# A two-layer mLSTM, GLA and sparse-attention block: projections with rows on partitions in 512 columns, weights kept by pieces, gates and w_out by blocks of rows

## Chip, cores and metric

The kernel runs on one core of a Trainium2 chip. The metric is the time of one execution in microseconds on the device, as the median of several runs. The engines are named as in the profile: PE (TensorE, with PEld for its weight loads), DVE (VectorE), ACT (ScalarE), POOL (GpSimd), SP (SyncE, which issues most of the DMAs).

## The reference

x has 512 rows (S) of 1024 (D_MODEL). Each of two layers does the following, all in float32; `split_columns` cuts the 9312 columns of the product with w_in by name.

```python
COLUMN_LAYOUT = (
    ('ml_q', 1024), ('ml_k', 1024), ('ml_v', 1024), ('ml_o', 1024), ('ml_z', 1024),
    ('ml_i', 4), ('ml_f', 4),
    ('gla_q', 256), ('gla_k', 256), ('gla_v', 512), ('gla_a', 16), ('gla_r', 512),
    ('dsa_q', 512), ('dsa_k', 512), ('dsa_v', 512), ('dsa_z', 512),
    ('idx_q', 512), ('idx_k', 64), ('idx_w', 8))

def hybrid_layer(x, ...):
    p = split_columns(rmsnorm(x, norm_g) @ w_in)
    qk = silu(causal_dwconv(concatenate([p['ml_q'], p['ml_k']]), ml_conv_w, ml_conv_b))
    mq, mk = split(qk, 2)
    hm = mlstm_chunkwise(heads(mq, 4), heads(mk, 4), heads(p['ml_v'], 4), li, lf)
    hm = hm * sigmoid(heads(p['ml_o'], 4))
    y_ml = rmsnorm(hm, ml_norm_g) * silu(p['ml_z'])
    la = log_sigmoid(p['gla_a'] @ gla_w_a + gla_b_a) / 16
    hg = gla_chunked(heads(p['gla_q'], 4), heads(p['gla_k'], 4), heads(p['gla_v'], 4), heads(la, 4))
    y_gla = rmsnorm(hg, gla_norm_g) * silu(p['gla_r'])
    dq, dk = rmsnorm(heads(p['dsa_q'], 4), dsa_q_g), rmsnorm(heads(p['dsa_k'], 4), dsa_k_g)
    hd = dsa_sparse_attention(dq, dk, heads(p['dsa_v'], 4), iq, p['idx_k'], iw, rel_bias, 128)
    y_dsa = hd * silu(p['dsa_z'])
    return x + concatenate([y_ml, y_gla, y_dsa]) @ w_out          # w_out: 2048 x 1024
```

The sparse attention scores all keys with the index heads, keeps the best 128 of each query, and attends to those with a relative bias.

## The kernel before

**Products.** Every float32 matrix product is made of three float32r products (`mm3`): a value is cut into a high part (hi) and the rest (lo), and hi x hi, hi x lo and lo x hi are summed in PSUM. x, after its norm, is transposed 128 rows at a time (`norm_in`: xs is the scaled block, psx its transposes, xhi and xlo the two parts with the 1024 inputs on partitions, 8 pieces k of 128).

**Two kinds of projection.** `proj_t` (PSUM tile pt) has the weights as the stationary operand: output columns on partitions, 512 rows of x streaming (384 in one case). It serves ml_q, ml_k, gla_q, gla_k and the index columns. `proj_n` (PSUM tile pn) has a block of 128 rows of x as the stationary operand and streams 256 weight columns, so that the rows lie on partitions; two blocks of rows stand side by side in one PSUM tile of 512. It serves ml_v, ml_o, ml_z, gla_v, gla_r and the four dsa groups, each in groups of 256 columns. Per group, pair of row blocks (pr), block (j) and k there are three matmuls. `chunks_two` does the same for the two gla_v groups, block by block, since the blocks of x become ready one after the other.

**Weights.** They are packed on the host in the order of use (`group_order`); a group is two halves of 128 x 1024 (512 KB each). A half is loaded by SP into a tile of the tag "w" (5 tiles: raw and lo), copied to float32r by ACT into the tag "hi" (4 tiles), and DVE subtracts (lo = raw - hi). `load`, `split`, `split_part`, `finish_split`, `take` and `done_with_group` keep this going: the next group's halves are split while one group is used, and tiles come back by whole groups.

**Order of the work.** A layer first does gla_v, the small columns (misc), idx_q and the GLA queries and keys, then goes through PLAN: ml heads 0 to 2, then "close" ml_z of heads 0 and 1, and so on; a close step is a gate (`y_group`: two groups of z, tanh, gating, transposes psy, parts yhi and ylo) followed by a quarter of the product with w_out (`w_out_part`, PSUM tile pw, 512 columns streaming, result added to xr). The recurrent and attention parts are background tasks: generators cut into stages that are issued between the projections' matmuls. Every engine call passes through `Meter.call`, which books it on an estimated clock of each engine (`Clock`), and at each `tick` the class `Background` issues the stages that should be ready by that clock, by priority. So the order in each engine's queue is fixed when the program is built, and all operations carry the same line, L180, in the profile. Tiles of 4 KB per partition come from the tag t4 (9), 2 KB from t2 (19), 8 KB from f8 (2).

**Names in the rows.** pn, pt, pw: see above; psx with xs, xhi, xlo: transposes of x; psy: transposes of a gated branch, of which so is mLSTM's, gv GLA's and dsa_v the attention's; cacc: the causal convolution of ml_q and ml_k (on DVE in threes); psq with qn: transposed dsa queries and keys; bs: relative bias with selection; pskd with kdn, and psst: GLA's state update; qz, psga: GLA's products inside a chunk.

Of the kernel before, what the change touches and what calls it, by code (L numbers as in the profile page):

```python
# [64 lines left out]

def group_order():
    order = []

    def cols(name, g=0):
        order.append(("in", OFF[name] + 256 * g))  # L70

    def out(q):
        order.append(("out", 512 * q, 0))
        order.append(("out", 512 * q, 512))

    def unit(kind, g):
        if kind == "dsa":
            for n in ("dsa_q", "dsa_k", "dsa_v"):
                cols(n, g)
        else:  # L80
            for n in ML_ORDER:
                cols(n, g)

    def steps(plan):
        for step in plan:
            if step[0] == "close":
                for g in range(2):
                    cols(step[1], step[2] + g)
                out(step[3])
            else:  # L90
                unit(*step)

    cols("gla_v", 0)
    cols("gla_v", 1)
    order.append(("misc",))
    cols("idx_q", 0)
    cols("idx_q", 1)
    order.append(("gqk", 0))
    order.append(("gqk", 1))
    steps(PLAN)  # L100
    return order


ML_ORDER = ("ml_o", "ml_q", "ml_k", "ml_v")
PLAN = (("ml", 0), ("ml", 1), ("ml", 2), ("close", "ml_z", 0, 0), ("ml", 3), ("close", "gla_r", 0, 2), ("dsa", 0), ("dsa", 1), ("close", "ml_z", 2, 1), ("close", "dsa_z", 0, 3))


def pack_weights(w_in, w_out):
    order = group_order()
    pack = np.zeros((DEPTH, len(order), 128, 2048), w_in.dtype)  # L110
    for layer in range(DEPTH):
        for i, spec in enumerate(order):
            dst = pack[layer, i]
            if spec[0] == "in":
                w = w_in[layer, :, spec[1]:spec[1] + 256]
                dst.reshape(128, KT, 256)[:] = w.reshape(KT, 128, 256).transpose(1, 0, 2)
            elif spec[0] == "gqk":
                d = dst.reshape(128, KT, 2, 128)
                for b, name in enumerate(("gla_q", "gla_k")):
                    w = w_in[layer, :, OFF[name] + 128 * spec[1]:OFF[name] + 128 * spec[1] + 128]  # L120
                    d[:, :, b, :] = w.reshape(KT, 128, 128).transpose(1, 0, 2)
            elif spec[0] == "out":
                w = w_out[layer, spec[1]:spec[1] + 512, spec[2]:spec[2] + 512]
                dst.reshape(128, 4, 512)[:] = w.reshape(4, 128, 512).transpose(1, 0, 2)
            else:
                d = dst[:, 0:1024].reshape(128, KT, 128)
                for name, n, at in MISC:
                    w = w_in[layer, :, OFF[name]:OFF[name] + n]
                    d[:, :, at:at + n] = w.reshape(KT, 128, n).transpose(1, 0, 2)
                dst[:, 0:1024] = d.reshape(128, 1024)  # L130
    return pack
# [34 lines left out]
class Meter:  # L166
    """Passes instructions on to an engine and books them on the engine's estimated clock (us)."""
# [98 lines left out]
class Background:  # L266
    """Tasks cut into stages: a stage is issued once what the stage before it made should be there."""
# [65 lines left out]
def hybrid_kernel(ctx, tc, a, out, dbg=None):  # L333
# [15 lines left out]
    N_T4, N_T2, N_F8, VA_BUFS = 9, 19, 2, 1  # L349
    W_BUFS, LOAD = 5, 4.5  # L350
# [19 lines left out]
    def t4(name, n=1024):  # L370
        return wk.tile([128, 1024], F32, tag="t4", name=name, bufs=N_T4)[:, 0:n]
# [3 lines left out]

    def f8(name):
        return wk.tile([128, 2048], F32R, tag="f8", name=name, bufs=N_F8)
# [35 lines left out]
    # (scale * mean + scale * eps) ** -0.5  # L413
# [4 lines left out]
    # two float32r parts of a value in PSUM, with a gain per partition and block: high first, low a stage later  # L418
# [23 lines left out]
    # one tag holds what was loaded and the low parts; a slot of it stays free while halves wait to be split  # L442
    order = [(layer, i) + spec for layer in range(DEPTH) for i, spec in enumerate(group_order())]
    halves_of = [1 if spec[2] == "misc" else 2 for spec in order]
    to_load = [(k, half) for k in range(len(order)) for half in range(halves_of[k])]
    loaded, ready, parts, half_done = {}, {}, [], []
    state = {"held": 0, "split": 0, "used": 0, "done": 0}

    def load(limit):
        while to_load and state["held"] < limit:  # L450
            state["held"] += 1
            k, half = to_load.pop(0)
            layer, i = order[k][:2]
            raw = wp.tile([128, 1024], F32, tag="w", name=f"raw{k}_{half}", bufs=W_BUFS)
            nc.sync.dma_start(raw, a["w_pack"][layer, i, :, 1024 * half:1024 * half + 1024])
            loaded[k, half] = (raw, clock.at["pe"] + LOAD)

    def split():
        k = state["split"]
        if k == len(order):  # L460
            return
        state["split"] += 1
        ready[k] = [], []
        for half in range(halves_of[k]):
            parts.append((k,) + loaded.pop((k, half)))

    def split_part():
        if half_done:
            k, raw, hi = half_done.pop()
            lo = wp.tile([128, 1024], F32R, tag="w", name=f"lo{k}", bufs=W_BUFS)  # L470
            nc.vector.tensor_sub(lo, raw, hi.bitcast(F32))
            n = {"misc": 128, "out": 512}.get(order[k][2], 256)
            for w, t in zip(ready[k], (hi, lo)):
                w.extend(t[:, c:c + n] for c in range(0, 1024, n))
            if not parts and state["split"] >= state["done"] + 2:
                load(W_BUFS)
        if parts and parts[0][2] <= clock.at["pe"]:
            k, raw, _ = parts.pop(0)
            hi = wp.tile([128, 1024], F32R, tag="hi", name=f"hi{k}", bufs=4)
            nc.scalar.activation(hi, raw, AF.Copy)  # L480
            half_done.append((k, raw, hi))

    def finish_split(k):
        while any(p[0] <= k for p in parts + half_done):
            if not half_done:
                clock.at["pe"] = max(clock.at["pe"], parts[0][2])
            split_part()

    def take(kind, at=None):
        k = state["used"]  # L490
        assert order[k][2] == kind and (at is None or order[k][3] == at), (order[k], kind, at)
        state["used"] += 1
        finish_split(k)
        return ready.pop(k)

    def done_with_group():
        finish_split(state["split"] - 1)
        state["held"] -= halves_of[state["done"]]
        state["done"] += 1
        load(W_BUFS - 1)  # L500
        split()
# [3 lines left out]
    def tick():  # L505
        split_part()
        bg.tick()
# [6 lines left out]
    def proj_t(w, blk, s0=0):  # L514
        wh, wl = w
        ps = pp("pt")
        c = slice(128 * blk, 128 * blk + 128)
        for k in range(KT):
            mm3(ps[:, s0:S], wh[k][:, c], wl[k][:, c], xhi[:, k, s0:S], xlo[:, k, s0:S], k == 0, k == KT - 1)
# [4 lines left out]
    def proj_n(w, pair):  # L524
        ps = pp("pn")
        for j in range(2):
            proj_n_half(ps, w, pair, j)
            if j == 0:
                tick()
        return ps  # L530

    def proj_n_half(ps, w, pair, j):
        wh, wl = w
        s = slice(128 * (2 * pair + j), 128 * (2 * pair + j) + 128)
        o = ps[:, 256 * j:256 * j + 256]
        for k in range(KT):
            mm3(o, xhi[:, k, s], xlo[:, k, s], wh[k], wl[k], k == 0, k == KT - 1)
            if k % TICK_K == TICK_K - 1 and k < KT - 1:
                tick()
# [816 lines left out]
```

## Time and profile before

| | |
|---|---|
| three runs | 1235.89, 1237.62, 1238.03 us; median 1237.62 |
| profiled execution, span | 1236.4 us |
| PE busy | 1215.7 us (98%) |
| DVE busy | 830.5 us (67%) |
| ACT busy | 583.2 us (47%) |
| POOL busy | 162.0 us (13%) |
| DMA | 107.98 MB, 87 GB/s mean |

The page tells the busy time of each engine and the chain of work that ended last. For the length of a matmul the start times of neighbours count, since matmuls overlap: the busy time of one is longer than the distance to the next. A bracket at the end of a timeline row, as [0.67 <-DVE lo], is the idle time of the engine before that row and what ended it. The page gives the execution's span and no other time of it; the median of the runs lies 1.2 us above the span.

### The profile page before, as it was taken

What the parts mean: (1) busy time and instruction counts of PE and PEld (TensorE: products, weight loads), DVE (VectorE), ACT (ScalarE), POOL (GpSimd) and SP (SyncE); (2) the same over time, 40 slices, a digit from 0 to 9 for tenths busy, and PEclk for the clock granted to TensorE, in tenths of its full rate; (3) what the DMA queues carried; (4) which work ended last, traced back from release to release, by engine and by line L of the source; (5) the groups of instructions that cost most, each with busy time, mean ns of one, the idle gap of its engine ahead of it and who ended that gap; (6) DMA issues with size and microseconds to landing.
All of it is one profiled execution on the core that took longest, in us unless ns stands there. A gap on an engine that the chain in (4) does not pass through costs nothing.

```text
span 1236.4 us, 20867 instructions
## 1 busy us (share of the span) xinstructions
PE 1215.7 (98%) x8308; PEld 1095.3 (89%) x8308; DVE 830.5 (67%) x1618; ACT 583.2 (47%) x1214; POOL 162.0 (13%) x293
## 2 busy tenths in 40 slices
PE   6999999999999999999999999999999999999998
PEld 6978889899889898998898889898988998989997
DVE  5479869796887844364556978888888875234643
ACT  6564546444153265542357544564442443554321
POOL 2003112300000013200010121031210000122000
PEclk9999999999999999999999999999999999999999
DMA  4333222222222223323223223122222322313222
GB/s 160 107 108 100 87 69 78 69 78 69 83 97 96 76 71 109 112 69 102 69 70 120 69 71 106 57 93 77 69 67 71 111 69 92 123 52 116 67 83 102
DMA packets 35169, 107.98 MB, mean 87 GB/s; under 512 B 5028, under 2 KB 8388, under 8 KB 35072
## 3 DMA queue, kind: packets, MB, share of 16 engines
q1 hardware_dynamic: 33136, 104.89, 26.0%
q8 instruction: 65, 1.06, 0.4%
q0 software_dynamic: 1200, 1.36, 0.3%
q10 hardware_dynamic: 736, 0.41, 0.1%
q14 instruction: 32, 0.26, 0.1%
HBM read 104.48 MB, written 3.43 MB: 87 GB/s over the span
## 4 chain that ended last, share of the span: by engine, by line
PE 93%; DVE 2%; ACT 2%; DMA 1%; POOL 1%; issue 1%; SPq 0%; DVEq 0%; POOLq 0%
PE pn L180 42%; PE pt L180 22%; PE pw L180 14%; PE psS L180 2%; PE pom L180 2%; PE pod L180 2%; PE psga L180 1%; PE pss L180 1%; PE pog L180 1%; PE psy L180 1%; DMA bs<-skew 1%; POOL bs L180 1%; PE psl L180 1%; DVE lo L180 1%; ACT xhi L180 1%
## 5 line engine op out<-in xcount | busy, mean ns | idle before, releaser
L180 PE MATMUL pn<-hi,xhi 128*128 128x256 f32 x1536 | 445.2, 290 | 0.0
L180 PE MATMUL pn<-hi,xlo 128*128 128x256 f32 x1536 | 434.4, 283 | 1.0 <-DVE xlo L180 1.0
L180 PE MATMUL pn<-lo,xhi 128*128 128x256 f32 x1536 | 433.6, 282 | 1.3 <-DVE lo L180 1.3
L180 DVE TENSOR_TENSOR lo<-raw,hi 128x1024 fp32r<-128x1024 f32 x178 | 221.9, 1247 | 184.4 <-ACT hi L180 178.1
L180 PEld LDWEIGHTS pn<-lo,xhi 128*128 128x128 f32 x1536 | 291.6, 190 | 4.0 <-DVE lo L180 1.7
L180 PEld LDWEIGHTS pn<-hi,xhi 128*128 128x128 f32 x1536 | 289.9, 189 | 4.4 <-PE psl L180 1.0
L180 PEld LDWEIGHTS pn<-hi,xlo 128*128 128x128 f32 x1536 | 290.3, 189 | 1.5 <-DVE xlo L180 1.5
L180 ACT ACTIVATE hi<-raw 128x1024 fp32r<-128x1024 f32 x178 | 188.1, 1057 | 117.2 <-DMA raw<-w_pack 89.4
L180 PE MATMUL pt<-xhi,hi 128*128 128x512 f32 (+1 forms) x400 | 158.8, 397 | 0.0
L180 PE MATMUL pt<-xlo,hi 128*128 128x512 f32 (+1 forms) x400 | 154.5, 386 | 0.0
L180 PE MATMUL pt<-xhi,lo 128*128 128x512 f32 (+1 forms) x400 | 154.5, 386 | 0.0
L180 PE MATMUL pw<-hi,yhi 128*128 128x512 f32 x256 | 102.2, 399 | 0.0
L180 PE MATMUL pw<-hi,ylo 128*128 128x512 f32 x256 | 101.6, 397 | 0.0
L180 PE MATMUL pw<-lo,yhi 128*128 128x512 f32 x256 | 101.4, 396 | 0.0
L180 PEld LDWEIGHTS pt<-xhi,hi 128*128 128x128 f32 x400 | 75.2, 188 | 17.6 <-issue 4.2
L180 PEld LDWEIGHTS pt<-xhi,lo 128*128 128x128 f32 x400 | 75.3, 188 | 15.3
L180 PEld LDWEIGHTS pt<-xlo,hi 128*128 128x128 f32 x400 | 75.4, 189 | 12.6
L180 DVE TENSOR_TENSOR xr<-pw,xr 128x512 f32<-128x512 f32 x64 | 44.1, 689 | 51.0 <-PE pw L180 50.9
L180 DVE SCALAR_TENSOR_TENSOR cacc<-cbuf,pv,cacc 128x512 f32<-128x512 f32 x96 | 74.5, 776 | 2.5 <-ACT cacc L180 0.2
L180 ACT ACTIVATE th<-pn 128x512 f32<-128x512 f32 x32 | 19.2, 599 | 86.7 <-PE pn L180 86.7
L180 PEld LDWEIGHTS pw<-hi,ylo 128*128 128x128 f32 x256 | 48.2, 188 | 12.6 <-DVE ylo L180 1.2
L180 ACT ACTIVATE cbuf<-pt 128x512 f32<-128x512 f32 x32 | 19.1, 597 | 84.0 <-PE pt L180 79.7
(187 smaller groups left out, 1694.9 us busy)
## 6 DMA issues: line engine op xcount, KB each, us to landing
raw<-w_pack SPq DMA_DIRECT2D x178, 512.0 KB, 3.9
xr<-x SPq DMA_DIRECT2D x4, 512.0 KB, 7.7
negm<-negm SPq DMA_DIRECT2D x8, 256.0 KB, 5.2
bs<-skew SPq DMA_DIRECT2D x8, 256.0 KB, 6.1
out_dram<-xr SPq DMA_DIRECT2D x8, 256.0 KB, 2.0
bs<-skew SPq DMA_DIRECT2D x8, 192.0 KB, 6.3
skew<-flat POOLq DMA_DIRECT2D x1, 1280.0 KB, 17.9
bs<-skew SPq DMA_DIRECT2D x8, 128.0 KB, 5.5
```

Source lines behind the costliest of these rows:

```text
L180: return f(*args, **kw)
```

## The change

1. `wide` takes the place of `proj_n`, `chunks_n`, `chunks_two` and `keep_n`. A wide step is two groups of 256 columns side by side, so that one matmul streams 512 columns for one block of 128 rows (sb). The groups paired are gla_v 0 and 1, ml_o and ml_v of a head, dsa_q and dsa_k of two heads, dsa_v 0 and 1, and the two groups of every close step. Blocks 0 and 1 each go through the four weight pieces (two k's each); blocks 2 and 3 alternate piece by piece, and a piece is given back after block 3. For gla_v all four blocks go one after the other (`before` drains the norm of the block).
2. Weights are kept as `Piece`s of 128 x 1024 with one tag "w" of 11 tiles for raw, hi and lo, of which at most 3 are raw (`make_room`, `prepare`, `need`, `take`, `give_back`). The tags "hi" and f8 are gone; t4 has 11 tiles, from which iq, ik, ml_q, ml_k, yhi and ylo now come.
3. What follows a projection works by block of rows for both groups: `y_part` (gate), `qk_part` (query and key norm), the evacuations of gla_v and dsa_v, gate and values of mLSTM. The mLSTM head's order is q, k, (o, v) instead of o, q, k, v; the dsa order is q and k of group 0, v of both, q and k of group 1.
4. `w_out_part` runs by pairs of row blocks: both halves of the columns for blocks 0 and 1, then both for 2 and 3, and each block waits for its own gate task only. Before, all four blocks went through the first half, then the second.

```diff
+    def make_room(most=RAWS):
+        while to_load and state["raw"] < most:
+            if state["used"] + 1 > W_BUFS - (2 if any(p.hi is None for p in wanted) or not held else 0):
+                break
...
+    def prepare():
         if half_done:
...
+            p = half_done.pop()
+            lo = w_tile("lo", F32R)
+            nc.vector.tensor_sub(lo, p.raw, p.hi.bitcast(F32))
+            state["used"] -= 1
+            state["raw"] -= 1
...
+            make_room()
+        if to_split and to_split[0].loaded <= clock.at["pe"] and state["used"] + 2 <= W_BUFS:
+            p = to_split.pop(0)
+            state["used"] += 2
+            p.hi = w_tile("hi", F32R)
+            nc.scalar.activation(p.hi, p.raw, AF.Copy)
+            half_done.append(p)
...
+    def wide(pieces, f, before=None):
+        pss = {}
+
+        def part(sb, i):
+            if i == 0:
+                if before:
+                    before(sb)
+                pss[sb] = pp("pn")
+            s = slice(128 * sb, 128 * sb + 128)
+            wh, wl = need(pieces[i])
+            for j in range(2):
+                k = 2 * i + j
+                mm3(pss[sb], xhi[:, k, s], xlo[:, k, s], wh[j], wl[j], k == 0, k == KT - 1)
+            if sb == NB - 1:
+                give_back()
+            if i == 3:
+                f(sb, pss.pop(sb))
             tick()
...
+        lone = NB if before else NB - 2
+        for sb in range(lone):
+            for i in range(4):
+                part(sb, i)
+        if not before:
+            for i in range(4):
+                for sb in range(lone, NB):
+                    part(sb, i)
...
-            for half in range(2):
-                if half:
-                    ws.append(take("out", 512 * q))
-                for sb in range(NB):
-                    chunk(sb, half)
...
+            for pr in range(2):
+                for half in range(2):
+                    for sb in (2 * pr, 2 * pr + 1):
+                        chunk(sb, half)
...
-        def keep_gv(g, pr, ps):
-            nc.scalar.activation(gv[g][:, 2 * pr:2 * pr + 2, :], blocks(ps, 2), AF.Copy)
+        def keep_gv(sb, ps):
+            for g in range(2):
+                nc.scalar.activation(gv[g][:, sb, :], ps[:, 256 * g:256 * g + 256], AF.Copy)
...
-        chunks_two("gla_v", keep_gv, lambda sb: bg.drain(norms[sb]))
+        wide(take("wide", OFF["gla_v"]), keep_gv, lambda sb: bg.drain(norms[sb]))
```

In the whole program the matmuls of pn go from 4608 with 256 columns to 2304 with 512.

ACT at the start of the program, from the last weight copy of the first group on. Before (zw is a part of the GLA gate's weights, gv the evacuation of the first projection):

```order
L180 ACTIVATE hi_184<-raw_0_115 128x1024
L180 ACTIVATE xs,rx<-xr 128x1024
L180 ACTIVATE hi_203<-raw_1_117 128x1024
L180 ACTIVATE zw<-wa 16x256 x2
L180 ACTIVATE xs<-xr,rx 128x1024
L180 ACTIVATE xhi<-psx,pv 128x128 x8
L180 ACTIVATE xs<-xr,rx 128x1024 x2
L180 ACTIVATE gv<-pn 128x512
L180 ACTIVATE xhi<-psx,pv 128x128 x16
```

and in the changed kernel, from the same operation on (xs,rx squares block 1 of x):

```order
L178 ACTIVATE xs,rx<-xr 128x1024
L178 ACTIVATE zw<-wa 16x256 x2
L178 ACTIVATE gv<-pn 128x256 x2
L178 ACTIVATE xs<-xr,rx 128x1024 x2
L178 ACTIVATE xhi<-psx,pv 128x128 x8
L178 ACTIVATE xs<-xr,rx 128x1024
L178 ACTIVATE xhi<-psx,pv 128x128 x16
```

The evacuation gv of block 0 moved ahead of the scaling xs of blocks 1 and 2, and the fourth copy of weights moved up, out of this stretch.

PE around GLA's state update (pskd and psst) of the first pair of heads of a layer. Before:

```order
L180 MATMUL pskd<-ident,za 128x128 x3
L180 MATMUL pt<-xhi,hi_986 128x512
L180 MATMUL pt<-xlo,hi_986 128x512
L180 MATMUL pt<-xhi,lo_1005 128x512
L180 MATMUL pt<-xhi,hi_986 128x512
L180 MATMUL pt<-xlo,hi_986 128x512
L180 MATMUL pt<-xhi,lo_1005 128x512
L180 MATMUL psst<-gv,kdn 64x128 x6
```

and in the changed kernel:

```order
L178 MATMUL pt<-xhi,hi 128x512
L178 MATMUL pt<-xlo,hi 128x512
L178 MATMUL pt<-xhi,lo 128x512
L178 MATMUL pskd<-ident,za 128x128 x3
L178 MATMUL psst<-gv,kdn 64x128 x6
L178 MATMUL pt<-xhi,hi 128x512
```

The six projections that stood between pskd and psst are now ahead of pskd.

DVE in the changed kernel during the first head's convolutions, numbers kept (acc3 with m8 is the search for the best keys):

```order
L178 SCALAR_TENSOR_TENSOR cacc_1694<-cbuf_1691,pv_112,cacc_1694 128x512 x3
L178 MAX m8_1745<-acc3_638 128x8
L178 MATCH_REPLACE acc3_638<-m8_1745,acc3_638 128x512
L178 MAX m8_1748<-acc3_638 128x8
L178 MATCH_REPLACE acc3_638<-m8_1748,acc3_638 128x512
L178 TENSOR_TENSOR lo_1757<-raw_1456,hi_1737 128x1024
L178 TENSOR_TENSOR lo_1790<-raw_1586,hi_1774 128x1024
L178 TENSOR_TENSOR ml_q_1525<-cacc_1598,ml_q_1524 128x512
```

and before, in the same stage (dec and qz belong to GLA):

```order
L180 SCALAR_TENSOR_TENSOR cacc_1290<-cbuf_1287,cacc_1290 128x512
L180 SCALAR_TENSOR_TENSOR cacc_1354<-cbuf_1351,pv_112,cacc_1354 128x512 x3
L180 COPY_PREDICATED att_1211<-lev_106,psga_1381 64x8x2x16 x2
L180 TENSOR_TENSOR ml_q_1235<-cacc_1290,ml_q_1234 128x512
L180 TENSOR_TENSOR lo11_1429<-raw11_0_1358,hi11_1413 128x1024
L180 TENSOR_TENSOR dec_1297<-dec_1297,gk_705 128x32x8
L180 TENSOR_TENSOR qz1_101<-dec_1297,gq_704 64x256 x2
```

Two lo's of the changed kernel stand next to each other behind a convolution triple and a search step; before, other work lies between one lo and the next.

## Rows read from the trace of the kernel before

**Rows 1.** The page: busy us (share) and instructions; the chain that ended last.

```profile
PE 1215.7 (98%) x8308; PEld 1095.3 (89%) x8308; DVE 830.5 (67%) x1618; ACT 583.2 (47%) x1214; POOL 162.0 (13%) x293
...
PE 93%; DVE 2%; ACT 2%; DMA 1%; POOL 1%; issue 1%; SPq 0%; DVEq 0%; POOLq 0%
```

**Rows 2.** PE's waits: us in total, times, longest us.

```profile
PE psx L180 <- ACT xs L180: 9.5, 1, 9.5
PE psq L180 <- ACT qn L180: 2.8, 2, 2.0
PE pn L180 <- DVE lo L180: 1.3, 2, 0.7
PE pn L180 <- DVE xlo L180: 1.0, 2, 0.7
PE psga L180 <- DVE qz L180: 0.8, 2, 0.6
PE psy L180 <- DVE dsa_v L180: 0.6, 2, 0.3
PE psy L180 <- DVE so L180: 0.5, 2, 0.2
```

**Rows 3.** The page's groups: busy us, mean ns of one, then idle before and releaser.

```profile
L180 PE MATMUL pn<-hi,xhi 128*128 128x256 f32 x1536 | 445.2, 290 | 0.0
...
L180 DVE TENSOR_TENSOR lo<-raw,hi 128x1024 fp32r<-128x1024 f32 x178 | 221.9, 1247 | 184.4 <-ACT hi L180 178.1
...
L180 ACT ACTIVATE hi<-raw 128x1024 fp32r<-128x1024 f32 x178 | 188.1, 1057 | 117.2 <-DMA raw<-w_pack 89.4
```

**Rows 4.** Chain of waits, long pieces of PE: start us, us, what.

```profile
313.42 15.25 PE pw L180 x64
...
948.89 22.49 PE pt L180 x96
...
1184.99 11.52 PE pn L180 x96
```

**Rows 5.** Windows (behind a wait, ml, dsa): busy us by engine, PEclk, DMA share.

```profile
1090.00:1094.00 4.00, 4.00 (x24) 4.00 (x23) 0.35 (x1) 0.91 (x3) 0.00 (x0) 0.57 0.05 11
...
175.00:325.00 150.00, 149.88 (x1048) 134.18 (x1048) 123.15 (x231) 75.89 (x164) 26.73 (x47) 1.00 0.22 71
...
425.00:550.00 125.00, 123.81 (x977) 118.09 (x976) 58.61 (x167) 65.37 (x189) 24.13 (x32) 1.00 0.29 93
```

**Rows 6.** Chain of waits at the start, between two projections.

```profile
19.24 0.45 PE psx L180 x4
...
19.72 0.48 ACT xhi L180 x2
...
20.89 0.36 DVE xlo L180
...
21.30 2.90 PE pn L180 x22
```

**Rows 7.** ACT's timeline at the start: start us, us, operation.

```profile
21.73 2.24 ACT L180 ACTIVATE xs<-xr,rx 128x1024 f32<-128x1024 f32 x2
24.23 0.60 ACT L180 ACTIVATE gv<-pn 128x512 f32<-128x512 f32 x1 [0.27 <-PE pn L180]
```

**Rows 8.** DVE's timeline in an ml stretch.

```profile
185.80 1.23 DVE L180 TENSOR_TENSOR lo<-raw,hi 128x1024 fp32r<-128x1024 f32 x1 [0.90 <-ACT hi L180]
186.94 2.32 DVE L180 SCALAR_TENSOR_TENSOR cacc<-cbuf,pv,cacc 128x512 f32<-128x512 f32 x3
```

**Rows 9.** PE's timeline at the border between the layers.

```profile
626.75 0.39 PE L180 MATMUL pn<-lo,xhi 128*128 128x256 f32 x1 [0.67 <-DVE lo L180]
...
630.01 0.39 PE L180 MATMUL pn<-lo,xhi 128*128 128x256 f32 x1 [0.68 <-DVE lo L180]
```

**Rows 10.** The operations on tile pskd: ns min/median/max, first and last start.

```profile
L180 ACT ACTIVATE kdn<-pskd x4: 471/486/492, 112.3 to 834.7; 128x384 f32<-128x384 f32 x4
```

**Rows 11.** Chain of waits around the bias sums of the second layer.

```profile
1081.26 4.83 POOL bs L180 x6
...
1087.50 1.28 ACT qn L180 x4
```

More of the change, by code (lines that the diff above doesn't have):

```diff
@@ L96, in group_order, with wide @@
[L96 to L100, printed above, removed]
-    return order
-ML_ORDER = ("ml_o", "ml_q", "ml_k", "ml_v")
-PLAN = (("ml", 0), ("ml", 1), ("ml", 2), ("close", "ml_z", 0, 0), ("ml", 3), ("close", "gla_r", 0, 2), ("dsa", 0), ("dsa", 1), ("close", "ml_z", 2, 1), ("close", "dsa_z", 0, 3))
+    def wide(*names):
+        order.append(("wide",) + tuple(OFF[n] + 256 * g for n, g in names))
+    wide(("gla_v", 0), ("gla_v", 1))
@@ new lines, in group_order @@
+    order.append(("misc",))
+    for g in range(2):
+        order.append(("in", OFF["idx_q"] + 256 * g))
+    for g in range(2):
+        order.append(("gqk", g))
+    for kind, *args in PLAN:
+        if kind == "ml":
+            for n in ("ml_q", "ml_k"):
+                order.append(("in", OFF[n] + 256 * args[0]))
+            wide(("ml_o", args[0]), ("ml_v", args[0]))
+        elif kind == "dsa_qk":
+            wide(("dsa_q", args[0]), ("dsa_k", args[0]))
+        elif kind == "dsa_v":
+            wide(("dsa_v", 0), ("dsa_v", 1))
+        else:
+            wide((args[0], args[1]), (args[0], args[1] + 1))
+            order.append(("out", 512 * args[2]))
@@ L108, in pack_weights @@
+    return order
+PIECES = {"wide": 4, "out": 4, "in": 2, "gqk": 2, "misc": 1}
+WIDTH = {"wide": 512, "out": 512, "in": 256, "gqk": 256, "misc": 128}
 def pack_weights(w_in, w_out):
     order = group_order()
-    pack = np.zeros((DEPTH, len(order), 128, 2048), w_in.dtype)
+    pack = np.zeros((DEPTH, sum(PIECES[spec[0]] for spec in order), 128, 1024), w_in.dtype)
     for layer in range(DEPTH):
[L112 to L124, printed above, removed]
-            else:
[L126 to L130, printed above, removed]
@@ L439, in split_task @@
             low_part(ps, hi, lo)
[L443 to L467, printed above, removed]
-        if half_done:
[L469 to L481, printed above, removed]
@@ L494, in take, with give_back @@
[L494 to L501, printed above, removed]
+        spec, pieces = units[state["unit"]]
+        assert spec[0] == kind and (at is None or spec[1] == at), (spec, kind, at)
+        state["unit"] += 1
+        wanted.extend(pieces)
+        held.extend(pieces)
+        return pieces
+    def give_back():
+        p = held.pop(0)
+        wanted.remove(p)
+        state["used"] -= 2
+        make_room()
@@ L518, in proj_t @@
         for k in range(KT):
-            mm3(ps[:, s0:S], wh[k][:, c], wl[k][:, c], xhi[:, k, s0:S], xlo[:, k, s0:S], k == 0, k == KT - 1)
+            n = KT // len(pieces)
+            wh, wl = need(pieces[k // n])
+            mm3(ps[:, s0:S], wh[k % n][:, c], wl[k % n][:, c], xhi[:, k, s0:S], xlo[:, k, s0:S], k == 0, k == KT - 1)
+            if last and k % n == n - 1:
+                give_back()
             if k % TICK_T == TICK_T - 1 and k < KT - 1:
@@ L522, in proj_t @@
         return ps
[L524 to L539, printed above, removed]
@@ L724, in y_group, with part @@
         def y_group(name, hns, g0=0):
             yt, tasks = [], []
-            def part(g, pr, ps):
-                tasks.append(bg.start(y_part(yt, hns[g], ps, 2 * g, pr), "y"))
-            for g in range(2):
-                chunks_n(name, g0 + g, lambda pr, ps: part(g, pr, ps))
+            def part(sb, ps):
+                tasks.append(bg.start(y_part(yt, hns, ps, sb), "y"))
+            wide(take("wide", OFF[name] + 256 * g0), part)
             return yt, tasks
         def w_out_part(q, yt, tasks, after=None):
-            ws = [take("out", 512 * q)]
+            pieces = take("out", 512 * q)
```

331 lines of the change are left out of this document (159 added, 172 removed).

## The prediction

> **What bounds the kernel now.** I read the page's busy times and chain first, then TensorE's waits, the page's costliest groups, and the long pieces of the chain. TensorE is busy for 1215.7 of 1236.4 us, and 93% of the chain that ended last is its matmuls; VectorE and ScalarE stand at 67% and 47% [rows 1]. So time is won or lost in two ways only: the columns that TensorE streams take another time, or TensorE waits more or less. The waits of TensorE sum to 16.5 us, of which 9.5 us is the first load, and the rest is a handful of waits under 1 us and two of about 1.4 us [rows 2]. The profile shows no recurring wait in the middle stretch that the change could remove. What a column costs is read from long undisturbed runs of matmuls in the chain of waits, since the busy time of one matmul (290 ns for 256 columns, [rows 3]) contains the overlap with its neighbours. There, 96 matmuls of 256 columns take 11.52 us (120.0 ns each) and 96 of 512 columns take 22.49 us (234.3 ns each) [rows 4]. Both are at full clock: the granted clock is 1.00 in the wide stretches, and lower in a stretch of 4 us behind one wait [rows 5].
>
> **Columns (the gain).** The change turns 4608 matmuls of 256 columns (three forms of 1536, of which [rows 3] shows one) into 2304 of 512. Two small ones cost 240.0 ns, one wide one 234.3 (22.49 / 96 = 0.23427), so each pair saves 5.73 ns, and 2304 pairs **-13.2 us**. The bound on the other side is the slowest 512-column run in the chain, 64 matmuls in 15.25 us, 238.3 ns [rows 4]: then 1.7 ns x 2304 = -3.9 us. I take the first, because the run of projections (pt) with 512 columns and the same three products, back to back, is nearest to what the new ones are; the slower run is in w_out, between whose chunks other work stands.
>
> The Trainium skill (TensorE: Matmul & The Clock Gate, "Wait — 56ns, not 53.3ns?") puts a warm matmul at columns by 2.4 GHz plus about 2.5 ns whatever its width. By that, two halves would differ from one whole by the 2.5 ns alone, and the gain would be 2304 x 2.5 = 5.8 us, an estimate from that page. The rows here give 120.0 and 234.3 ns and so a larger fixed part; the measurement decides, and the sum does without the page.
>
> **The start.** Before, ScalarE scales block 1 of x ahead of the first evacuation of a projection, and TensorE loses 2.06 us between its transposes of block 1 (19.24) and the next projection (21.30), [rows 6]. In the new order of ScalarE both evacuations of block 0's projection stand ahead of the scaling of blocks 1 and 2, and the evacuations wait for TensorE's last matmul of block 0. From that matmul on, the chain is: two evacuations (one of 512 columns takes 0.60, [rows 7]; two of 256 I put at 0.8), two scalings 2.24 [rows 7], the first half of xhi 1.15 (19.72 to 20.87) and xlo 0.36 [rows 6], and 0.5 for the handoffs: 5.0 us. Against 2.06, and less 0.43 for four transposes of block 2 that now lie inside the wait, that is **+2.5 us** (0 if the real wait is hidden as before, +3.5 if the fourth weight piece is late too).
>
> **Weights.** Loads are as many as before, 178 of 512 KB, with the same 178 hi copies on ScalarE (1057 ns) and lo differences on VectorE (1247 ns) [rows 3]. What changes is when they are issued. Before, two groups' worth of halves lie ready and lo of a half is in most cases issued 6 us or more ahead of its first use. Now a piece must find a free slot of 11, and counted in TensorE's new order 27 of 178 have 3.1 us or less between lo's issue and first use (12 before); 22 of these are the last piece of a wide group, with 13 wide matmuls (3.04 us) ahead, and 18 (4.2 us) between hi's issue and use. The bare chain is hi 1.06 [rows 3] and lo 1.23 [rows 8], 2.3 us, which fits. It doesn't fit where a convolution triple of 2.32 us stands ahead of lo on VectorE [rows 8]: 1.06 + 2.32 + 1.25 = 4.6 us, 0.4 us over. VectorE is busy 82% in the ml stretch but 47% in the dsa stretch [rows 5], so I count the eight ml_o with ml_v pairs, take six of them as hit: 6 x 0.4 = **+2.5 us**. Bounds: 0 (all hidden; before, 12 with such leads gave two waits) and 27 x 0.4 = +11. Behind a late lo nothing but TensorE itself waits; its later background work comes later by the same amount.
>
> **At the layer border** two waits for lo, 0.67 and 0.68 us [rows 9], came from both new blocks' transposes being squeezed between first-use pieces. With w_out by blocks of rows, the norms of blocks 0 and 1 are issued half a w_out earlier, and the wide group's pieces are prepared before: **-1.3 us** (-1.3 to 0).
>
> **Small waits.** (a) w_out's chunks take the halves of a pair of row blocks together, so the gated rows 2 and 3 have four chunks of 12 x 0.234 (11.2 us) as cover instead of two (5.6); the wait psy for so disappears, **-0.5** [rows 2]. The transposes for dsa, gated per block, now follow the last dsa_v product by 1.4 us for five groups instead of two; at 0.3 us each, as the rows have it [rows 2], **+0.9** (0 to 2.5). (b) In the gla stage pskd is directly followed by psst once a layer, where six projections (1.4 us) stood between; psst needs ScalarE's kdn, 0.486 us [rows 10], and with handoffs I put it at 0.8 each: **+1.6** (0 to 2.4). (c) gla's qz waits (0.8 now, [rows 2]): **+0.5** (0 to 2). (d) psq's wait (2.0 us at the longest, [rows 2]) comes behind POOL's bias sums, 4.83 us in the chain [rows 11]; the matmuls in front of it are in the same arrangement of psl, projections and psst, so I take 0, with 1.7 either way, since the granted clock behind that wait sank to 0.57 over 4 us [rows 5].
>
> **Costs taken as nothing:** 120 more small ScalarE and 80 more VectorE operations (evacuation, gating and norms by block) lie on engines with 53% and 33% free [rows 1]. They are hidden by TensorE's projections; without that cover the ScalarE ones, at up to the 0.60 us of a 512-column evacuation [rows 7], would be 72 us. Stores and tail are as before.
>
> **The sum.** -13.2 + 2.5 + 2.5 - 1.3 + 0.9 - 0.5 + 1.6 + 0.5 = -7.0. Against the profiled execution of 1236.4 that is 1229.4; the median of the three runs lies 1.2 above that span, so **1230.6 us**.
>
> **Rivals.**
> A, everything hidden: the planner's cover suffices, the start chain overlaps, and only the columns and the vanished waits count: 1236.4 - 13.2 - 1.8 + 1.2 = 1223. For it: TensorE waits almost nowhere now, though 12 pieces have short leads. Against it: the order on ScalarE at the start leaves little room.
> B, the fixed cost per matmul is smaller than the runs suggest: at 238.3 ns the gain is 3.9 us instead of 13.2, and with the same added waits of 6.2 the time is 1236.4 - 3.9 + 6.2 + 1.2 = 1240, or 1238 if the waits are a third lower. For it: the spread of 512-column runs, 234.3 to 238.3 [rows 4]. By the fixed 2.5 ns of the page named above the same sum would be 1238, on this side too.
> C, just-in-time weights take the gain and more (slower): every last piece of a group waits, because its hi can be written only once TensorE gives back the slot, and VectorE has work queued. Without my lo term the forecast is -9.5; it ends over +2.5 (0.2%) when lo waits pass 12.0 us, that is 0.44 us on each of 27 pieces. At 0.7 us each, as the lo waits at the border show [rows 9], it is 18.9 us and 1236.4 - 9.5 + 18.9 + 1.2 = 1247. For it: ScalarE's hi is already what VectorE waits for, in 178 of its 184 us before lo [rows 3]. Against it: the new chain of 2.3 us fits into 3.04 to 4.2.
>
> **How the numbers follow.** Forecast, 1226 to 1235: 0.50. A: 0.18. B: 0.10. C: 0.16. No net effect through something not seen here: 0.06. A measurement of this kernel can tell about 0.2% from no change, so faster means under 1235.1 and slower over 1240.1: faster 0.68, same 0.16, slower 0.16. The bounds all at their low ends give 1221, at their high ends 1256. The range goes from 1220 (the low end less the scatter of 1 us of the runs), takes in A and B, and ends in the near part of C at 1242, which leaves most of C outside.
>
> **What would show it.** The pn matmuls should number 2304 and run at 234 ns start to start in an undisturbed stretch. In TensorE's waits, psx should have a second entry near 5 us, lo some ten entries of under 1 us, psst one or two for kdn, and the border's lo waits none. The forecast is wrong if pn runs at 238 ns or more (B), if lo waits sum to over 10 us (C), or if the granted clock sinks behind the new waits, which none of the terms contain.

## The result, and the profile after

The changed kernel takes 1229.86 us (median of 5 runs, 1229.35 to 1233.38), the kernel before, in the runs beside it, 1238.03 us (5 runs). The ratio is 0.9933, with a 95% interval from 0.9916 to 0.9951: faster by 8.2 us, clear of the noise. The forecast was 1230.6. The execution that was profiled took 1229.57 us with a span of 1227.9, so 1.7 us lie outside the span, where the prediction had put 1.2.

The page of the changed kernel, engines and three groups (busy us, mean ns of one, idle before and releaser); to be held against [rows 1] and [rows 3]:

```profile
PE 1200.6 (98%) x6004; PEld 970.6 (79%) x6004; DVE 836.3 (68%) x1698; ACT 601.7 (49%) x1334; POOL 165.3 (13%) x309
...
L178 DVE TENSOR_TENSOR lo<-raw,hi 128x1024 fp32r<-128x1024 f32 x178 | 219.4, 1232 | 171.1 <-ACT hi L178 169.2
L178 PE MATMUL pn<-hi,xhi 128*128 128x512 f32 x768 | 314.5, 410 | 0.0
...
L178 ACT ACTIVATE hi<-raw 128x1024 fp32r<-128x1024 f32 x178 | 188.7, 1060 | 197.1 <-PE pn L178 100.1
```

There are 768 matmuls of each form in place of 1536, as announced. The weight copy hi now waits for PE (100.1 us, the slot that is given back) where it waited for its DMA before [rows 3].

PE's waits in the changed kernel: us in total, times, longest. They sum to 23.4 us, against 16.5 [rows 2]:

```profile
PE psx L178 <- ACT xs L178: 10.3, 2, 8.4
PE psq L178 <- ACT qn L178: 3.5, 2, 1.8
PE pst L178 <- ACT bs L178: 2.7, 4, 0.9
PE pn L178 <- DVE lo L178: 2.5, 4, 1.3
PE psS L178 <- DVE ml_k L178: 1.6, 2, 0.9
PE pskd L178 <- DVE za L178: 1.4, 1, 1.4
PE psst L178 <- ACT kdn L178: 1.2, 2, 0.6
PE pod L178 <- ACT pT L178: 0.2, 1, 0.2
```

Long pieces of PE in the chain of the changed kernel (start us, us, what); they answer to [rows 4]:

```profile
933.96 22.48 PE pt L178 x96
956.44 14.01 PE pn L178 x60
...
1015.99 16.36 PE pw L178 x72
```

pn takes 14.01 / 60 = 233.5 ns, pt 234.2 as before. But pw takes 16.36 / 72 = 227.2 ns. In the kernel before, an undisturbed run of 72 of them reads

```profile
1020.73 16.86 PE pw L180 x72
```

which is 234.2 ns. The prediction did not have it that the matmuls of w_out, which keep their count and shape, would each become 7 ns shorter. Summed from start to start over the whole trace they fall from 181.6 to 176.6 us. In the 181.6 are 0.6 us that TensorE waited for dsa_v (psy, [rows 2]) right behind a matmul of w_out; without them the matmuls gave **4.4 us**, about half of the whole result. Much of what follows is about this.

### The profile page after: what moved, and what is told of

It is laid out like the page before. It is cut to its first block, busy times and chain, and to the rows that moved or that the text cites. A ratio compares the mean times of both kernels' runs of the same rounds, so it can differ in the third digit from the quotient of the medians.

```text
span 1227.9 us, 16538 instructions
## 1 busy us (share of the span) xinstructions
PE 1200.6 (98%) x6004; PEld 970.6 (79%) x6004; DVE 836.3 (68%) x1698; ACT 601.7 (49%) x1334; POOL 165.3 (13%) x309
## 5 line engine op out<-in xcount | busy, mean ns | idle before, releaser
L178 DVE TENSOR_TENSOR lo<-raw,hi 128x1024 fp32r<-128x1024 f32 x178 | 219.4, 1232 | 171.1 <-ACT hi L178 169.2
L178 PE MATMUL pn<-hi,xhi 128*128 128x512 f32 x768 | 314.5, 410 | 0.0
L178 PE MATMUL pn<-lo,xhi 128*128 128x512 f32 x768 | 306.2, 399 | 2.5 <-DVE lo L178 2.5
L178 PE MATMUL pn<-hi,xlo 128*128 128x512 f32 x768 | 305.0, 397 | 0.0
L178 ACT ACTIVATE hi<-raw 128x1024 fp32r<-128x1024 f32 x178 | 188.7, 1060 | 197.1 <-PE pn L178 100.1
L178 PEld LDWEIGHTS pn<-lo,xhi 128*128 128x128 f32 x768 | 145.5, 189 | 37.3 <-DVE lo L178 5.5
L178 PEld LDWEIGHTS pn<-hi,xlo 128*128 128x128 f32 x768 | 145.1, 189 | 35.5 <-DVE xlo L178 1.0
L178 PEld LDWEIGHTS pn<-hi,xhi 128*128 128x128 f32 x768 | 145.6, 190 | 32.9 <-PE psl L178 0.5
L178 DVE SCALAR_TENSOR_TENSOR cacc<-cbuf,pv,cacc 128x512 f32<-128x512 f32 x96 | 72.0, 750 | 2.5
L178 DVE MAX8 m<-acc 128x8 f32<-128x512 f32 (+2 forms) x96 | 53.5, 558 | 3.2 <-POOL acc L178 1.5
L178 PEld LDWEIGHTS pw<-lo,yhi 128*128 128x128 f32 x256 | 48.1, 188 | 9.5
```

What stands on the lines that cost most here:

```text
L178: return f(*args, **kw)
```

## Experiments

All are compared with 1229.86 us of the changed kernel, and each had the kernel before beside it (1238.6 to 1239.0 in those runs). The ratios are to the kernel before.

### Why w_out became faster: where the operands begin

What the change did to w_out's operands is to move them. Their tiles yhi and ylo came from the 8 KB tiles before, and come from the 4 KB tiles now. By the addresses that the built program gives its tiles, which stand in no trace, the starts modulo 512 bytes are:

| kernel | xhi, xlo | weights | yhi, ylo | distance in pn, pt | distance in pw |
|---|---|---|---|---|---|
| before | 224 | 320 | 416 | 96 | 96 |
| changed | 224 | 320 | 320 | 96 | 0 |

(pn and pw have x or y as the stationary operand and the weights streaming, pt the other way round. All steps inside these tiles are multiples of 512 bytes.) Four runs change the starts alone, with unused tiles as padding.

First run:

```diff
+    const.tile([128, 8], F32, name="pad0")
     xhi = const.tile([128, KT, S], F32R, name="xhi")
     xlo = const.tile([128, KT, S], F32R, name="xlo")
+    const.tile([128, 8], F32, name="pad1")
```

> The changed kernel with two unused tiles of 32 bytes per partition, one ahead of xhi and one behind xlo, so that xhi and xlo begin at multiples of 64 bytes (36064 and 52448 are 32 over one) and everything behind them keeps its place modulo 64. Why: w_out's matmuls run at 234 ns start to start before and 227 after; its stationary parts yhi and ylo moved from addresses 32 over a multiple of 64 to multiples of 64, as the weights are, while xhi and xlo are 32 over in both. Theory 1 (address): pn goes from 233.3 to about 227 ns (2304 x 6.6 = 15 us) and pt from 234 to about 227 (1008 x 7 = 7 us and a little in the 384 columns): about 1207 us. Theory 2 (the cadence belongs to the order of the product, w_out by pairs of blocks): pn and pt stay at 233 to 234, 1230 us.

Measured: 1227.93 us (ratio 0.9917, 0.9898 to 0.9935). Neither theory: the mean time from start to start in undisturbed stretches went from 233.4 to 232.6 ns for pn and from 233.9 to 232.6 for pt, not to 227. Modulo 64 the operands then stood alike, modulo 512 they were 128 apart.

Second run:

```diff
     make_room(2)
+    wp.tile([128, 8], F32, tag="pad", name="pad", bufs=1)
     params.append(load_parameters(0))
```

> The changed kernel with one unused tile of 32 bytes per partition behind the weights' tiles, so that all tiles of t4, yhi and ylo among them, begin 32 bytes over a multiple of 64; the weights, xhi and xlo keep their addresses. Theory 1 (address): pw goes from 227 back to about 234 ns, 768 x 6.5 = +5 us, 1235 us; pn and pt unchanged. Theory 2 (order of w_out): pw stays at 227, 1230 us.

Measured: 1233.85 us (0.9962, 0.9946 to 0.9979), 4.0 us more. Its chain shows pn as it was and pw slow again, 16.79 / 72 = 233.2 ns:

```profile
960.77 14.01 PE pn L178 x60
...
1020.37 16.79 PE pw L178 x72
```

The order of w_out's work is the same in both, so the address is the cause, and 32 bytes are enough.

Third run, the same tile ahead of the weights' tiles:

```diff
+    wp.tile([128, 8], F32, tag="pad", name="pad", bufs=1)
+
     def make_room(most=RAWS):
```

> The changed kernel with the unused tile of 32 bytes ahead of the weights' tiles: weights, yhi and ylo, xhi and xlo all begin 32 bytes over a multiple of 64. If what counts is that the two operands stand alike (relative), pn, pt and pw all run at 227 ns: 1230 - 22 = 1208 us. If each operand has to begin at a multiple of 64 (absolute), all are slow: pw 234, pn 233 or more, 1235 us or more. By theory 2 nothing moves, 1230 us.

Measured: 1227.28 us (0.9912, 0.9894 to 0.9929), neither of the two figures, since the tile also left pn and pt with a distance, 128 in place of 96. pw stays fast although weights, yhi and ylo all begin 32 bytes over a multiple of 64; pn and pt read as in the first run. Chain of waits, pt 233.2 and pw 227.5 ns:

```profile
932.23 22.39 PE pt L178 x96
...
1014.02 16.38 PE pw L178 x72
```

So it is the distance between the two operands that counts, not where each of them begins. Why it does, no run shows.

Fourth run, distance 0 everywhere (all four at 448 modulo 512):

```diff
+    lev = const.tile([128, len(LEVELS), 32], U8, name="lev")
     xhi = const.tile([128, KT, S], F32R, name="xhi")
     xlo = const.tile([128, KT, S], F32R, name="xlo")
+    const.tile([128, 32], F32, name="pad")
...
-    lev = const.tile([128, len(LEVELS), 32], U8, name="lev")
```

> The changed kernel with lev (224 bytes) moved ahead of xhi and an unused tile of 128 bytes behind xlo: xhi, xlo, the weights, yhi and ylo now all begin at 448 over a multiple of 512 bytes. The runs before showed that the distance between the two operands counts: alike, w_out's matmuls take 227 ns, 32 bytes apart 233; in the runs where xhi and the weights stood 128 bytes apart modulo 512, pn and pt went only from 233.3 and 233.8 to 232.6. Theory 1 (the distance counts modulo 512 or the like, as in w_out, where it is 0): pn and pt go to 227 ns, 2304 x 6.6 + 1008 x 7.1 = 22 us, about 1207 us. Theory 2 (64 or 128 bytes are all that counts, the rest belongs to the kind of product): as in the run with 64, 232.6 ns and 1228 us.

Measured: 1217.11 us (0.9823, 0.9808 to 0.9838), 12.75 us less than the changed kernel. All three kinds of product now run alike, 226.7, 226.7 and 226.9 ns by the chain:

```profile
924.23 21.76 PE pt L178 x96
945.99 13.60 PE pn L178 x60
...
1004.47 16.34 PE pw L178 x72
```

Theory 1 holds for the mechanism. The gain is less than its 22 us for two reasons that the trace shows. After an interruption up to some ten matmuls pass before the short time sets in, so the means are 228.0 (pn) and 228.5 (pt). Counted for each matmul from its start to the start of the next, less idle time and what half the clock cost, pn falls by 11.8 us and pt by 5.0, together 16.8. And the faster PE waits more: its waits grow from 23.4 to 27.1 us. 16.8 less 3.7 is 13.1; the spans differ by 13.3, the medians by 12.75.

Fifth run, the kernel before with the same edit:

> The kernel before with the same two edits, so that xhi and xlo begin alike with the weights modulo 512; yhi and ylo keep their distance from them. pt should go from 234 to 227 by theory 1 (1008 x 7 = -7 us). For the 256 columns of pn: if a matmul's loss by the distance is one per matmul, 4608 x 6.6 = -30 us more, 1201 us, and the wider matmuls of the change would be worth nothing; if it grows with the columns, 4608 x 3.3 = -15 us, 1216 us; if 256 columns are free of it, 1231 us. By theory 2 all stays at 1237 us.

Measured: 1232.47 us (0.9952, 0.9934 to 0.997), 6.5 us less than the kernel before in the same runs. Its chain:

```profile
945.13 21.79 PE pt L180 x96
966.92 17.27 PE pn L180 x144
...
1016.19 16.87 PE pw L180 x72
```

pt falls to 227.0 ns; pw, whose operands remain apart, stays at 234.3; pn with 256 columns stays at 119.9. So the 256-column matmuls were free of the loss on average, and the gain of the wider ones was held down by it: 2 x 119.9 - 233.5 = 6.3 ns a pair where the operands stand apart, 2 x 119.9 - 226.7 = 13.1 ns where they stand alike.

### What the columns are worth

```diff
+    def halved(ps, lh, ll, rh, rl, first, last):
+        for l, r in ((lh, rh), (lh, rl), (ll, rh)):
+            whole = first and l is lh and r is rh or last and l is ll
+            for c in (slice(0, 512),) if whole else (slice(0, 256), slice(256, 512)):
+                nc.tensor.matmul(ps[:, c], lhsT=l, rhs=r[:, c], start=first and whole, stop=last and whole)
...
-                mm3(pss[sb], xhi[:, k, s], xlo[:, k, s], wh[j], wl[j], k == 0, k == KT - 1)
+                halved(pss[sb], xhi[:, k, s], xlo[:, k, s], wh[j], wl[j], k == 0, k == KT - 1)
```

> The changed kernel with each 512-column matmul of a wide step cut into two of 256, save the first and the last of the 24 of a block: 2112 of 2304 become 4224 with 256 columns; order, pieces and background stay. If the gain of the prediction is that of the columns (2 x 119.9 against 233.3 ns, 6.5 ns a pair), the time rises by 2112 x 6.5 = 13.7 us to 1243 us. Rival: the columns are worth little and the gain came from w_out and the order, then 1230 to 1233 us.

Measured: 1241.05 us (1.0021, 1.0011 to 1.0031), 11.2 us more than the changed kernel. The columns were worth that much, and without them the change would have been slightly slower than before. Counted from start to start as for the fourth run, pn takes 11.8 us more in its trace, not the 13.7 of undisturbed stretches. The longer work also covers waits: PE's waits sum to 20.4 us there against 23.4 (lo 0.8 against 2.5, psq 2.3 against 3.5, psS 0.6 against 1.6). Two more stretches of 3.4 us at half clock in that execution cost about what those waits gave. Each matmul here has its own weight load, 8116 of both in that run against 6004, so the run doesn't tell the width from the number of loads.

The same cut with the operands alike:

> The changed kernel with both edits: operands alike modulo 512, and each wide matmul cut into two of 256 columns (2112 of 2304). Beside the run with 512 columns and the same addresses it gives what the width is worth where the distance costs nothing: 0 if two small ones cost as much as one wide one at 227 ns (113.4 each), 2112 x (2 x 119.8 - 227) = 27 us if 256 columns keep 119.8 ns.

Measured: 1235.41 us (0.9974, 0.9964 to 0.9985), 18.3 us over the run with 512 columns and the same addresses. That is between the two figures: pn takes 21.7 us more in the trace, waits 4.1 us less, and half clock costs 3.2 us more. The width and the addresses belong together: 11.2 us apart, 18.3 us alike.

### The start

In the changed kernel the chain at the start is the one that the prediction drew. ACT's timeline and then PE's (start us, us, operation, idle before and what ended it):

```profile
17.11 0.85 ACT L178 ACTIVATE zw<-wa 16x256 fp32r<-16x256 f32 x2 [2.50 <-DMA wa<-gla_w_a]
17.99 0.66 ACT L178 ACTIVATE gv<-pn 128x256 f32<-128x256 f32 x2
18.67 2.19 ACT L178 ACTIVATE xs<-xr,rx 128x1024 f32<-128x1024 f32 x2
```

```profile
19.87 1.97 PE L178 MATMUL psx<-ident,xs 128*128 128x128 f32 x12 [1.92 <-ACT xs L178]
21.49 0.78 PE L178 MATMUL pn<-hi,xhi 128*128 128x512 f32 x1
```

The evacuation gv stands ahead of the scaling xs, and PE waits for xs.

```diff
+    def scaled(sb):
+        while not norms[sb]["done"] and norms[sb].get("steps", 0) < 3:
+            bg.step(norms[sb])
...
             if i == 3:
+                if before and sb + 1 < NB:
+                    scaled(sb + 1)
                 f(sb, pss.pop(sb))
...
-        t_zw = bg.add(rank_weights())
+        t_zw = bg.add(rank_weights(), None, 0.0 if layer else 24.0)
```

> The changed kernel with another order on ScalarE at the start: the next block of x is scaled ahead of the evacuation of the projection of the block before, and the parts of the GLA gate's weights (zw) come later. In the changed kernel TensorE waits 1.92 us for the scaling of block 1, and the chain from its last projection of block 0 (17.9) to the next (21.5) is 3.6 us, against 2.1 before. If that wait is the order's, it goes and the chain returns to about 2 us: -1.5 us, 1228.3 us. Rival: the wait is that of the data (x or its norm late), then the time stays at 1229.9 us.

Measured: 1229.4 us (0.992, 0.9906 to 0.9935), no difference that can be told from 1229.86. In the trace the wait falls to 1.08 us and everything from 41 to 480 us comes 1.7 us earlier; the changed kernel then catches up. The windows (busy us of the engines, granted clock, DMA share, GB/s) show how, first of the changed kernel, then of this run:

```profile
22.00:26.00 4.00, 4.00 (x16) 2.96 (x15) 3.06 (x12) 3.96 (x13) 0.00 (x0) 0.68 0.00 2
492.00:496.00 4.00, 3.67 (x19) 2.74 (x20) 0.35 (x1) 3.29 (x10) 0.00 (x0) 1.00 0.02 4
```

```profile
22.00:26.00 4.00, 4.00 (x23) 3.32 (x22) 0.98 (x4) 2.19 (x4) 0.00 (x0) 1.00 0.00 0
492.00:496.00 4.00, 4.00 (x15) 3.54 (x16) 0.35 (x1) 1.70 (x5) 0.00 (x0) 0.57 0.02 4
```

The changed kernel's execution has a stretch at the lower clock behind the start and none at 492; the other has it the other way round. Both are 3.4 us at half the full clock, 1.7 us of work. So the lead of 1.7 us is that stretch and no more: of the order itself (the wait 0.84 us shorter, a new one of 0.44 us for xlo, restarts) nothing is left at 41 us. Whether the edit decides which pauses are followed by the low clock is not shown. The mean granted clock also differs between executions of one kernel: it was 0.992 to 0.997 in the five of the changed kernel.

### psq, and sums moved to another engine

In the changed kernel the norm rq of the last block stands behind eight bias sums on GpSimd, and ACT waits for it; the first two rows are POOL's timeline, then ACT's:

```profile
484.26 6.06 POOL L178 TENSOR_TENSOR bs<-bs,sel 128x512 f32<-128x512 f32 x8 [27.91 <-DMA bs<-skew]
490.40 0.19 POOL L178 TENSOR_SCALAR rq<-rq 128x4 f32<-128x4 f32 x1
```

```profile
491.73 1.28 ACT L178 ACTIVATE qn<-qn,rq 128x128 f32<-128x128 f32 x4 [3.42 <-POOL rq L178]
```

```diff
-            nc.gpsimd.tensor_tensor(bs, bs, selt[i], op=OP.add)
+            (nc.vector if hh else nc.gpsimd).tensor_tensor(bs, bs, selt[i], op=OP.add)
```

> The changed kernel with every second sum of bias and selection (bs) on VectorE in place of GpSimd. In the changed kernel the norm of the last block of dsa queries and keys (rq, 1.2 us on GpSimd) stands behind eight such sums (6.06 us), ScalarE waits 3.4 us for it, and TensorE then 1.75 us at psq, in each layer (0.8 and 2.0 before). If the sums are the cause, the psq waits go (3.5 us in all), and with them perhaps the stretch of 3.4 us at half clock that follows one of them (1.7 us): 1224.5 to 1226.5 us. Rival: TensorE then waits at the next place (the transposes of the probabilities, pst, 2.7 us now) for the sums that VectorE does later, and the time stays within 1 us of 1229.9.

Measured: 1230.72 us (0.9935, 0.9921 to 0.9949), the rival. psq's wait is gone, and pst's has grown from 2.7 to 8.1; PE's waits, then DVE's timeline:

```profile
PE psx L178 <- ACT xs L178: 11.1, 2, 8.2
PE pst L178 <- ACT bs L178: 8.1, 2, 4.1
```

```profile
485.94 0.91 DVE L178 TENSOR_TENSOR bs<-bs,sel 128x512 f32<-128x512 f32 x1 [5.11 <-DMA bs<-skew]
487.38 2.17 DVE L178 TENSOR_TENSOR bs<-bs,sel 128x384 f32<-128x384 f32 x3 [0.54 <-DMA bs<-skew]
```

VectorE now waits for the bias's DMA and does four sums before it comes to the maxima that the exponentials wait for. The profiled execution was the slowest of six (1232.97 us, mean granted clock 0.991, the others 0.994), with three stretches of 6.8 us at half clock where the changed kernel's had two of 3.4; in the other five, too, the clock was below the 0.996 to 0.997 of four of the changed kernel's five.

### The order of w_out

```diff
-            for pr in range(2):
-                for half in range(2):
-                    for sb in (2 * pr, 2 * pr + 1):
-                        chunk(sb, half)
+            for half in range(2):
+                for sb in range(NB):
+                    chunk(sb, half)
```

> The changed kernel with w_out in the order of before: all four blocks of rows through the first half of the columns, then through the second. The prediction gave the order by pairs 0.5 us for the gated so and 1.3 us at the border of the layers. If that was right, the psy waits for so come back (0.5 us) and the lo wait at the border (0.86 us left in the changed kernel) grows to 1.3 or more: 1231 to 1232 us. Rival: the border's lo wait has another cause and the order is worth nothing, 1229.9 us. The 227 ns of w_out's matmuls should stay either way, since the addresses stay.

Measured: 1234.83 us (0.9966, 0.9955 to 0.9977), 5.0 us more. The waits of PE that differ:

```profile
PE pw L178 <- DVE ylo L178: 3.3, 5, 1.0
...
PE pn L178 <- DVE lo L178: 1.6, 3, 1.2
```

w_out waits for ylo of the last gated blocks, 3.3 us that the order by pairs covers. The profiled execution, whose span is 6.0 us longer, also has two more stretches of 3.4 us at half clock than that of the changed kernel, which would be 3.4 us. How much of the 5.0 us is the order's own is therefore between 3.3 us, less what the border gains, and the whole. pw kept its 227 ns. And the lo wait at the border of the layers (0.86 us in the changed kernel) is absent here: with the old order there is none, so there the order by pairs costs.

### Together

> Operands alike modulo 512 bytes (1217.1 us alone) and the order at the start (1229.4 alone; in its trace 1.7 us ahead of the changed kernel up to 480 us, and level with it after a stretch of 3.4 us at half clock that the changed kernel's profiled execution did not have there). If the start's gain is real and the half clock comes by chance, 1215.4 us; if a wait moved in time brings a half-clock stretch each time, 1217.1.

Measured: 1215.33 us (0.9812, 0.9795 to 0.9829), the figure for a start that is worth 1.7 us; one of its four runs took 1217.20. It beats both kernels, by 23 us the one before. The traces don't show a steady gain of the start, though. TensorE's rows in the run with alike operands alone:

```profile
20.12 1.79 PE L178 MATMUL psx<-ident,xs 128*128 128x128 f32 x12 [3.63 <-ACT xs L178]
...
130.93 0.50 PE L178 MATMUL pn<-lo,xhi 128*128 128x512 f32 x1 [1.38 <-DVE lo L178]
```

and in this run:

```profile
19.10 1.10 PE L178 MATMUL psx<-ident,xs 128*128 128x128 f32 x8 [1.47 <-ACT xs L178]
```

Its wait for xs is shorter and no half clock follows, so it is 1.86 us ahead at 90 us. A stretch at half clock from 116 us on leaves 0.33 us of that, and then the wait of 1.38 us for lo at 131 us isn't there, and the lead is back at 1.85 us. So this stretch cost little, since it covered a wait that followed.

> As the run before, and with every second bias sum on VectorE. If the three gains add: 1215.4 less 3.5 to 5.2, 1210 to 1212 us; if the bias sums are worth nothing, as the run with the order at the start.

Measured: 1215.84 us (0.9815, 0.9798 to 0.9832): the bias sums on VectorE bring nothing here either; psq's wait is gone and pst's is 8.6 us.

## Why the prediction was right

The time was right, and the main term too. That the whole came out within 1 us was partly luck: what the sum lacked or mis-sized went both ways and nearly cancelled. The matmuls are counted from start to start, less idle time and what half the clock cost.

| step of the sum | predicted | shown by the two traces |
|---|---|---|
| columns of pn | -13.2 | -14.8 (undisturbed: 2304 x (240.0 - 233.5) = -15.0) |
| cadence of w_out | 0 | -4.4 |
| all other matmuls | not in the sum | +2.3 (psq +1.0, pt +0.9, pst +0.6, pskd +0.5, psy -1.0, others) |
| waits at the start (psx) | +2.5 | +0.8: a new wait of 1.9, the first load 1.1 earlier |
| lo, in the ml stretch and elsewhere | +2.5 | +1.6 (1.25, 0.17, 0.17) |
| lo at the border | -1.3 | -0.5 (one wait of 0.86 remains) |
| psy: so, dsa_v | -0.5, +0.9 | -0.5, -0.6 |
| kdn | +1.6 | +1.2 |
| qz | +0.5 | -0.8 |
| psq | 0 | +0.7 |
| pst, psS, pskd, pod, xlo | not in the sum | +2.7, +1.6, +1.4, +0.2, -1.0 |
| half clock behind the start | not in the sum | +1.7 |

The entries come to -8.4 us; the spans differ by 8.5. The waits grew by 6.9 us, where the sum had 6.2, but that agreement is luck: the waits that the sum has came to 1.9 us, and waits that it doesn't have to 4.9. TensorE's columns and w_out gave 6.0 us more than forecast, and half clock, the other matmuls and 0.5 us more outside the span (1.7 against 1.2) took 4.5 of it back.

**Columns.** The step was right: 120.0 and 234.3 ns were read from the right rows (pn now takes 233.5), and the run that cut the columns again gave 11.2 us. The rule of the Trainium skill that had been set beside it (TensorE: Matmul & The Clock Gate, "Wait — 56ns, not 53.3ns?") would make a pair save 2.5 ns. The runs show 6.3 or 13.1 ns, by how the operands stand, so the measurement decides against that rule for this float32r stream. Rival B, which rested on a 512-column run at 238.3 ns, took a disturbed run for a property; the undisturbed run of 72 in the same chain has 234.2.

**w_out's cadence** is the step that was missing. I took the matmuls of w_out as untouched because their shapes, count and operands' layout inside a tile were. The change moved their tiles, and each matmul went from 234.2 to 227.2 ns; no row of the trace of before can show what that does.

**Waits.** The mechanism of the weights was right where it was placed. At 130 us VectorE has a convolution triple ahead of two lo's; VectorE's timeline, then PE's, where also the border's wait stands:

```profile
128.27 2.32 DVE L178 SCALAR_TENSOR_TENSOR cacc<-cbuf,pv,cacc 128x512 f32<-128x512 f32 x3
130.51 2.53 DVE L178 TENSOR_TENSOR lo<-raw,hi 128x1024 fp32r<-128x1024 f32 x2
```

```profile
131.78 0.50 PE L178 MATMUL pn<-lo,xhi 128*128 128x512 f32 x1 [1.25 <-DVE lo L178]
...
626.36 0.50 PE L178 MATMUL pn<-lo,xhi 128*128 128x512 f32 x1 [0.86 <-DVE lo L178]
```

It hit one head hard and two lightly, not six at 0.4 us: rival C was far off. At the border the reason given (norms issued earlier through the order by pairs) fails, since the old order has no wait there. The order by pairs itself was mis-sized at 0.5 us: with gates by blocks of both groups the last gates end late, and it covers 3.3 us of ylo. psq's place was right, a bound of 1.7 held its 0.7; its two waits before, read as two of about 1.4 us, were one of 2.0 and one of 0.8. One of the signs of being wrong did show: the granted clock sank behind the new wait at the start, at a cost of 1.7 us that no term held. The new wait itself was 1.9 us, not the second entry near 5 us. Three waits that the sum didn't name (for bs, ml_k and za) add 5.7 us. That a faster PE exposes what the slower one covered is shown by the run with narrow columns, where the psS wait falls from 1.6 to 0.6; what exposes pst and za in particular was not tried.

## What to carry to other kernels

Where matmuls with a float32r weight load each stream 512 columns, look at where the two operands' tiles begin in SBUF: with the starts alike modulo 512 bytes a matmul took 227 ns here, otherwise 232 to 234, and on top of the rewrite some bytes of padding were worth 12.75 us, more than the rewrite itself (on the kernel before, 6.5 us). Read the cadence as start to start in a long undisturbed run of each kind of product, before and after; when it moves for a product that no edit names, see whether its tiles' addresses have moved. On an engine that is busy 98% of the time, expect part of a gain in its own work to come back as waits (here 3.7 of 16.8 us with the operands alike, 6.9 of 19.2 in the change), and a gain of 1.7 us to be told only by several runs, because each 3.4 us at half clock weighs as much.

## What the runs showed of the hardware

- The distance between the starts of the stationary and the streaming operand sets the cadence of 512-column float32r products: in long undisturbed runs of the chain 0 modulo 512 bytes gave 226.7 to 227.6 ns, 32 gave 233.2 to 233.5, 96 gave 233.3 to 234.4, 128 gave 232.3 to 233.3. Both starts 32 bytes over a multiple of 64 are as fast as both at one. Other distances, and whether a smaller period than 512 would do, were not tried. With 256 columns (119.9 against 120.0 ns at distances 0 and 96) nothing changed, nor with the 384 of some pt (174.7 against 174.4 ns on average). The Trainium skill (SBUF — State Buffer, "Operand start alignment") asks of an operand's start only a multiple of its element size, and says of its measurements that they timed nothing; every start here is such a multiple, and the runs show that where it lies does matter for time.
- The cadence is not reached at once. Behind an interruption the times from start to start of w_out's matmuls scatter between 224 and 236 ns for up to some ten matmuls and are then 227, 226, 227 without a break.
- Which pauses are followed by 3.4 us at half clock differs from trace to trace: behind the start, near 117 us behind the waits for za and kdn, behind psq of either layer, or behind several of them; with the bias sums on VectorE three stretches were 6.8 us long. Since the mean granted clock also differs between executions of one kernel, no run shows that an edit decides it.
